# A hybrid decoder step: convolution output and sample unit moved into the chain over token tiles

## The chip, the cores and the metric

The kernel runs on one core of a Trainium2 chip. The metric is the device time of one execution in microseconds (us); of several runs the median counts. The engines are named as in the profile: PE is TensorE (matmuls; PEld its weight loads), DVE is VectorE, ACT is ScalarE, POOL is GpSimd, SP is SyncE, which here only issues DMAs.

## The reference

One inference step through two layers, for a prompt of 1024 tokens and for 8 sample sequences of 8 tokens that come with their own states. Everything is in float32; the model width is 1024.

```python
# layer 0
proj = x @ w_in                                   # 1024 -> 2816
u = value * sigmoid(gate)                         # half A: 512 channels
a = silu(layer_norm(causal_conv_31_taps(u) + b))
# half B: 8 heads of 64; token shift, low-rank decay, gates
for t in tokens:                                  # state S: 64 x 64 for each head
    S = S * w_t + (S @ a_t) * b_t + v_t * k_t
    o_t = S @ r_t
b = (group_norm(o) + bonus) * g
mix = concat(a, b) @ w_out
# layer 1
mix = causal means over 2, 4, 8, 16 tokens, minus x, then @ pool_w
# after each of the two
x = layer_norm(ALPHA * x + mix)
x = layer_norm(ALPHA * x + (silu(x @ wg) * (x @ wu)) @ wd)   # 1024 -> 2816 -> 1024
```

The outputs are x for both kinds of tokens and the new states of convolution, token shift, matrix S and pooling.

## The kernel before

The 1088 tokens are nine tiles, 0 to 7 with 128 prompt tokens each and 8 with the 64 sample tokens. A product in float32 is made of three matmuls on high and low parts, each operand being split into the two (`split`; `mm`, L75, issues a matmul). All engines but one take their order from an automatic planner that goes by priority, which is program order unless `high_priority` shifts it; TensorE's order is the planner's too in phase 1 and in the first part of phase 2, and from `manual_schedule` in `phase2` on it is program order. PSUM has four tags, mm, o, ch and tp, of two buffers each.

*Phase 1* (`phase1`, L219 to L388) makes the projection in 22 output tiles. Its sequence is `ORDER` (L180). An entry c0 to c3 is a convolution tile of two projections, gate (evicted by ScalarE) and value (evicted by VectorE, L293), and then 31 taps over 1024 prompt tokens on VectorE (L305 to L312), issued at a low priority (`LATE`); the few sample taps are products on POOL (L320) with a reduction on VectorE. The result goes to DRAM (`accd`, L323). The entries 20 and 21 are the low-rank inputs, 16 to 19 are v, 12 to 15 k, and 8 to 11 r, for the head pairs p0 to p3. When k and r of a pair are there, `prep` makes that pair's operands in three blocks of tokens, and `invert(p)` (L643 to L666) inverts the triangular matrices of the pair, in 31 steps of two instructions each, a product into `xt` and a sum into `X`. Its tiles have one buffer, so the four pairs are inverted one after another, p0 and p3 on POOL, p1 and p2 on VectorE (`PINV`). The result goes to DRAM.

*Phase 2* (`phase2`, L934 to L1027) turns this into the mixed output. The convolution's share is `convs`, eleven slots: slot x transposes tile x of `accd` and normalises it (`conv_a`, names `cl`, `cz`), makes the output product of tile x-2 with the upper half of `w_out` (`wout` with `wA`, names `wo`, `ahl`, `y`), and transposes back with the activation (`conv_b`, names `clt`, `yh`). The first eight slots are emitted ahead of the chain, under the planner's order for TensorE; three follow in units 0 to 2.

The chain goes over units 0 to 7, one for each prompt tile. `load_unit` brings a unit's operands from DRAM; `unit_pe` makes its transposes and merges the inverted blocks (the first is `pT`, L749); `chain` makes the dependent steps, two chunks of 64 tokens each, and between them calls `fill`, which takes further work for TensorE from the queue `fq`: the next unit's `unit_pe`, convolution slots, the step `gn` of the unit before (`gn_out`: group norm on VectorE, then gate), and tails. `tail(i)` is the output product of tile i with the lower half of `w_out` (`wB`, from the gated result `bt`) and the layer norm (`normalize`). `xt(i)` transposes a finished tile for the FFN. Units 3 to 7 take tails 0 to 5 and the `xt` of tiles 0 to 4. The sample's matrices are inverted by `invert(None)`, emitted after unit 0; `chain_sample` (four functions, s0 to s3, for each pair) begins in unit 7 and stands mostly behind it, together with tails 6, 7 and 8. `wB` is loaded after unit 2 with its split on POOL (L91). The nine `y` tiles stay in SBUF, and `xt` of tiles 7 and 8 is done beside the first FFN products.

After it come the FFN of layer 0, the pooling layer and its FFN, which are matmuls from weights that are streamed in.

Of the kernel before, what the change touches and what calls it, by code (L numbers as in the profile page):

```python
# [17 lines left out]
D = 1024  # L18
# [43 lines left out]
class Prog:  # L62
# [77 lines left out]
    def xt(self, l, i, y, pool, tag):  # L140
# [38 lines left out]
    CONV0 = 8  # L179
    ORDER = ("c0", "c1", 20, 21, 16, 12, 8, "c2", 17, 13, 9, "c3", 18, 14, 10, 19, 15, 11)  # L180
# [4 lines left out]
    CAUTO = 8  # L185
# [7 lines left out]
    def consts(self, es, e1):  # L193
        tc, nc, I = self.tc, self.nc, self.I
        pool = lambda name, bufs=1, **kw: es.enter_context(tc.tile_pool(name=name, bufs=bufs, **kw))
        self.pp = pool("psum", 2, space=PSUM)
# [8 lines left out]
        self.c1d = [[self.dr.tile([128, TH], F32, name=f"c1d{l}_{x}") for x in range(NF)] for l in range(2)]  # L205
        self.hd = [[self.dr.tile([128, TOK], F32, name=f"hd{l}_{f}") for f in range(NF)] for l in range(2)]
# [12 lines left out]
    def phase1(self):  # L219
# [13 lines left out]
        pool = lambda name, bufs=1, **kw: es.enter_context(tc.tile_pool(name=name, bufs=bufs, side="right", **kw))  # L233
# [38 lines left out]
        def conv_tile(ct):  # L272
# [33 lines left out]
            with tc.high_priority(offset=-self.LATE):  # L306
# [16 lines left out]
                nc.scalar.dma_start(out=self.accd[ct], in_=acc)  # L323
# [67 lines left out]
    def conv_a(self, i):  # L391
# [44 lines left out]
    def wout(self, i, get, w, alpha, after=None):  # L436
# [26 lines left out]
    def convs(self, wA):  # L463

        slots = []
        for x in range(11):
            out = []
            if x < 9:
                out += self.conv_a(x)
            if x >= 2:  # L470
                out += self.wout(x - 2, lambda j=x - 2: self.chl.pop(j), wA, ALPHA)
            if x < 9:
                out += self.conv_b(x)
            slots.append(out)
        return slots

# [191 lines left out]
    def load_unit(self, i):  # L668

        nc, up = self.nc, self.up  # L670
        u = type("Unit", (), {})()
        u.i, u.samp, u.nm = i, i == 8, f"t{i}"
# [7 lines left out]
        u.TT = up.tile([128, G, 64], F32, tag="TT", name=f"TT_{nm}")  # L680
# [8 lines left out]
        u.A21 = up.tile([128, G, 32], F32, tag="A21", name=f"A21_{nm}")  # L689
        u.ATm = [up.tile([128, G, 128], F32, tag=f"ATm{hd}", name=f"ATm{hd}_{nm}") for hd in range(2)]  # L690
# [49 lines left out]
    def merge(self, u):  # L740
# [5 lines left out]
        def one():  # L746
# [3 lines left out]
            t.T11 = up.tile([128, G, 32], F32, tag="T11", name=f"T11_{nm}", bufs=1)  # L750
# [92 lines left out]
    def gn_out(self, u, src, bts):  # L843
# [19 lines left out]
        def step():  # L863
# [12 lines left out]
            bts[u.i] = bt  # L876
        return step

    def chain_sample(self, u):
# [7 lines left out]
        S0, rS, w, pc = {}, {}, {}, {}  # L887
# [14 lines left out]
        def s1(p):  # L902
            pc[p] = self.psum("ch", f"spc{p}")
            for hd in range(2):
                self.mm(pc[p][H[hd], 0:64], ATm[hd][:, p, 0:64], SUV[:, 0, 0, hd, p])
            w[p] = self.wp_.tile([128, 4, 64], F32, tag="w", name=f"sw{p}")
            self.copy_act(w[p][:, 0], pc[p][:, 0:64])

        def s2(p):
            for hd in range(2):  # L910
                self.mm(pc[p][H[hd], 64:128], TTt[H[hd], p, :], w[p][H[hd], 0])
            self.copy_act(SUV[H[0], 0, 1, 0, p], pc[p][H[0], 64:128])
            nc.vector.tensor_copy(out=SUV[H[1], 0, 1, 1, p], in_=pc[p][H[1], 64:128])

        def s3(p):
            po = self.psum("o", f"spo{p}")
# [14 lines left out]

        return s0, s1, s2, s3, [Osb[:, hd].rearrange("p c v -> p (c v)") for hd in range(2)]

    def phase2(self):  # L934
        tc, nc, I, O = self.tc, self.nc, self.I, self.O
        es = ExitStack()
        pool = lambda name, bufs=1, **kw: es.enter_context(tc.tile_pool(name=name, bufs=bufs, side="right", **kw))
# [3 lines left out]
        self.tpool = pool("tmp2", 5)  # L941
# [22 lines left out]
        def xt(i):  # L964
            return self.xt(0, i, self.y[i], self.tpool, "t")

        self.fq, self.cz, self.chl = deque(), {}, {}
        bts, wB, gn = {}, [], {}
        wA = [self.load_w(I["w_out"][k], f"woA{k}", nc.vector) for k in range(4)]
        us = {0: self.load_unit(0), 1: self.load_unit(1)}  # L970
        slots = self.convs(wA)
        first = slots[:self.CONV0]
# [580 lines left out]
```

## Time and profile before

| | |
|---|---|
| Median of 3 runs | 2350.27 us (2343.52 to 2356.04) |
| Profiled execution | 2353.67 us, span 2351.9 us, mean granted clock 0.958 |
| PE busy | 2191.6 us, 93% of the span |
| PEld busy | 1971.6 us, 84% |
| DVE busy | 1558.9 us, 66% |
| ACT busy | 910.3 us, 39% |
| POOL busy | 449.3 us, 19% |
| DMA | 352.83 MB, mean 150 GB/s |

The span is the time from the first to the last instruction of the profiled execution; the busy times are sums over it. A busy share is an average over stages that have different limits, so it says little about a change in one stage. For that the stretch has to be cut out: busy time and granted clock in windows, and the order of the instructions of one engine with what ended each wait.

### The profile page before, as it was taken

How to read it: one execution, taken by the hardware profiler on the slowest of the kernel's cores; microseconds unless marked ns; L12 is line 12 of the kernel's file. 1: busy time of each engine (PE TensorE's matmuls, PEld its weight loads, DVE VectorE, ACT ScalarE, POOL GpSimd, SP SyncE). 2: the span in 40 equal slices, each digit the busy share in tenths (PEclk: the TensorE clock that was granted, in tenths of full speed). 3: DMA queues.
4: the chain of work that ended last, by engine and by line, in shares of the span. 5: the costliest groups of instructions: out<-in, count | busy, mean ns of one | idle time of the engine just before them, and what ended most of it. 6: DMA issues, size and time to landing. Idle time of an engine off the chain costs nothing.

```text
span 2351.9 us, 39322 instructions
## 1 busy us (share of the span) xinstructions
PE 2191.6 (93%) x15026; PEld 1971.6 (84%) x15026; DVE 1558.9 (66%) x2859; ACT 910.3 (39%) x2041; POOL 449.3 (19%) x551
## 2 busy tenths in 40 slices
PE   8898898869896899999999999989999999999998
PEld 7887787657664799999997787879999999977886
DVE  6987698734457535777767657455477777667565
ACT  3243244445642543333333434343443333334332
POOL 3588866563111000000000101000000000000010
PEclk9999899679998999999999999999999999999999
DMA  5132326745532654333348555444463333376662
GB/s 169 48 116 75 108 86 193 230 124 152 158 95 98 228 193 148 113 119 120 120 128 268 186 163 185 141 157 159 159 222 120 120 120 120 121 241 188 218 199 92
DMA packets 234362, 352.83 MB, mean 150 GB/s; under 512 B 73461, under 2 KB 151597, under 8 KB 234164
## 3 DMA queue, kind: packets, MB, share of 16 engines
q1 hardware_dynamic: 187294, 284.01, 39.1%
q10 hardware_dynamic: 46878, 66.30, 8.0%
q8 instruction: 118, 1.93, 0.3%
q14 instruction: 72, 0.59, 0.1%
HBM read 261.72 MB, written 88.74 MB: 149 GB/s over the span
## 4 chain that ended last, share of the span: by engine, by line
PE 60%; DVE 4%; DMA 4%; issue 2%; ACT 1%; SPq 0%; POOL 0%; ACTq 0%; POOLq 0%; DVEq 0%
PE dn L75 17%; DMA yr<-yd 1%; PE wo L75 1%; PE pp L75 1%; PE pl L75 1%; DMA b<-lnv 1%; PE pa_1u L75 1%; DVE op_d L96 1%; PE pa_10u L75 1%; PE pa_4g L75 1%; PE pa_2g L75 1%; PE pa_5g L75 1%; PE pa_3u L75 1%; PE pa_2u L75 1%; PE pa_3g L75 1%
## 5 line engine op out<-in xcount | busy, mean ns | idle before, releaser
L75 PE MATMUL dn<-op_d,h 128*128 128x512 f32 (+1 forms) x2288 | 544.7, 395 | 16.7 <-ACT op_d L72 6.6
L75 PEld LDWEIGHTS dn<-op_d,h 128*128 128x128 f32 (+1 forms) x2288 | 422.1, 187 | 117.9 <-DVE op_d L96 8.4
L75 PE MATMUL in<-xh,hl_in 128*128 128x384 f32 (+1 forms) x1056 | 282.5, 348 | 15.8 <-ACT xh L72 7.5
L104 POOL TENSOR_TENSOR rstd_f<-rs_f,mhalf 128x1 f32<-128x1 f32 (+1 forms) x18 | 36.3, 2017 | 1328.2 <-DVE rs_f L103 762.4
L96 DVE TENSOR_TENSOR op_d<-raw_d,op_d 128x512 fp32r<-128x512 f32 x264 | 179.2, 685 | 161.5 <-ACT op_d L72 161.0
L72 ACT ACTIVATE op_d<-raw_d 128x512 fp32r<-128x512 f32 x264 | 163.4, 625 | 292.4 <-PE dn L75 262.2
L75 PEld LDWEIGHTS in<-xh,hl_in 128*128 128x128 f32 x1056 | 199.0, 200 | 28.4 <-ACT xm L345 8.0
L312 DVE SCALAR_TENSOR_TENSOR acc<-u,hv,acc 128x1024 f32<-128x1024 f32 x120 | 193.2, 1619 | 0.8
L75 PE MATMUL in<-xl,hl_in 128*128 128x384 f32 (+1 forms) x528 | 182.7, 346 | 2.2 <-DVE xl L96 2.2
L75 PEld LDWEIGHTS in<-xl,hl_in 128*128 128x128 f32 x528 | 105.7, 200 | 5.4 <-DVE xl L96 2.9
L96 DVE TENSOR_TENSOR h<-hr,h 128x384 fp32r<-128x384 f32 (+2 forms) x176 | 72.8, 433 | 15.4 <-ACT h L72 15.4
L72 ACT ACTIVATE h<-hr 128x384 fp32r<-128x384 f32 (+2 forms) x176 | 69.2, 416 | 17.1 <-DMA hr<-hd 12.5
L156 ACT ACTIVATE xo<-xt,vec 128x128 f32<-128x128 f32 (+1 forms) x144 | 53.0, 452 | 44.1 <-PE xt L154 43.1
L75 PE MATMUL wo<-hl_woB,bhl 128*128 128x512 f32 (+1 forms) x216 | 65.0, 445 | 5.0 <-ACT bhl L72 4.9
L104 POOL TENSOR_TENSOR rstd_m<-rs_m,mhalf 128x1 f32<-128x1 f32 (+1 forms) x18 | 11.3, 629 | 271.2 <-DVE rs_m L103 264.7
L91 POOL TENSOR_TENSOR hl_in<-raw_in,hl_in 128x1024 fp32r<-128x1024 f32 x21 | 58.5, 2785 | 15.7 <-ACT hl_in L72 15.7
L75 PE MATMUL wo<-hl_woA,ahl 128*128 128x512 f32 (+1 forms) x216 | 57.6, 418 | 0.8 <-DVE y L456 0.4
L75 PEld LDWEIGHTS wo<-hl_woB,bhl 128*128 128x128 f32 (+1 forms) x216 | 41.2, 202 | 18.5 <-ACT bhl L72 6.0
L75 PEld LDWEIGHTS wo<-hl_woA,ahl 128*128 128x128 f32 (+1 forms) x216 | 40.6, 194 | 11.1 <-DVE y L456 0.7
L72 ACT ACTIVATE rw<-in 128x384 f32<-128x384 f32 (+2 forms) x56 | 22.0, 394 | 46.1 <-PE in L75 30.9
L75 PE MATMUL pl<-hl_pw,phl 128*128 128x256 f32 (+1 forms) x216 | 33.4, 286 | 3.3 <-DVE phl L96 2.8
L320 POOL TENSOR_TENSOR prod<-u,hv 128x496 f32<-128x496 f32 x16 | 30.6, 1915 | 29.9 <-DVE u L293 16.3
(1040 smaller groups left out, 4769.8 us busy)
## 6 DMA issues: line engine op xcount, KB each, us to landing
raw_d<-ffn_down SPq DMA_DIRECT2D x132, 512.0 KB, 3.8
hd<-sg ACTq DMA_DIRECT2D x88, 272.0 KB, 4.1
hr<-hd SPq DMA_DIRECT2D x88, 192.0 KB, 3.7
raw_in<-w_in SPq DMA_DIRECT2D x22, 512.0 KB, 4.3
xl<-xtd SPq DMA_DIRECT2D x16, 544.0 KB, 4.6
ATm_t<-atd SPq DMA_DIRECT2D x16, 512.0 KB, 5.3
yr<-yd SPq DMA_DIRECT2D x16, 512.0 KB, 5.7
xtd<-xo ACTq DMA_DIRECT2D x28, 256.0 KB, 3.7
```

The source lines that it names most:

```text
L72: self.nc.scalar.activation(out=out, in_=in_, func=AF.Copy)
L75: self.nc.tensor.matmul(out, lhsT, rhs, start=start, stop=stop, **kw)
L91: (eng or nc.gpsimd).tensor_tensor(out=hl[:, 1, :], in0=raw, in1=hl[:, 0, :].bitcast(F32), op=ALU.subtract)
L96: (eng or self.nc.vector).tensor_tensor(out=out_lo, in0=src, in1=out_hi.bitcast(F32), op=ALU.subtract)
L104: nc.gpsimd.tensor_tensor(out=out, in0=t[:P, :n], in1=self.mhalf[:P, :n], op=ALU.pow)
L156: nc.scalar.activation(out=xo[:, k, :n], in_=ps[:, k * 128:k * 128 + n], func=AF.Identity, scale=self.v("lng", 16 * l + 4 * q + k), bias=s ...
L312: nc.vector.scalar_tensor_tensor(out=out, in0=src, scalar=cw(j), in1=out, op0=ALU.mult, op1=ALU.add)
L320: nc.gpsimd.tensor_tensor(out=prod, in0=win, in1=taps, op=ALU.mult)
```

## The change

- `ORDER` puts c1 behind the tiles of p0 and c3 last. The store of `accd` is issued from SP instead of ACT.
- No slot of `convs` is emitted ahead of the chain. `SLOTS` puts two slots into unit 1 and three into each of units 2, 3 and 4; `manual_schedule` begins before the first unit, and `invert(None)` stands first.
- `y` has four buffers in place of nine tiles: after the convolution's share a tile is stored to DRAM (`store_y`) and read back before its tail (`load_y`); the gated `bt` goes the same way.
- The sample unit has its own buffers and is loaded in unit 0. Its transposes, s0, and s1 to s3 stand in units 4, 5 and 6, with s1 and s2 joined over the four pairs; its group norm is made in unit 7.
- `TAILS` and `XTS` place tail 0 in unit 5, tails 1 and 2 in unit 6, 3 and 4 in unit 7; behind the chain follow `gn[7]` and the tails 5, 8, 6, 7 with the `xt` of the other tiles between. `xt` of tile 8 is no longer beside the FFN.
- `wB` is loaded before unit 5, its split on VectorE. Some pools get `reuse_waits="tile"`, and `tmp2` has six buffers for five.

The diff, cut to its core:

```diff
-    ORDER = ("c0", "c1", 20, 21, 16, 12, 8, "c2", 17, 13, 9, "c3", 18, 14, 10, 19, 15, 11)
+    ORDER = ("c0", 20, 21, 16, 12, 8, "c1", 17, 13, 9, "c2", 18, 14, 10, 19, 15, 11, "c3")
...
-                nc.scalar.dma_start(out=self.accd[ct], in_=acc)
+                nc.sync.dma_start(out=self.accd[ct], in_=acc)
...
-                out += self.wout(x - 2, lambda j=x - 2: self.chl.pop(j), wA, ALPHA)
+                out += self.wout(x - 2, lambda j=x - 2: self.chl.pop(j), wA, ALPHA, lambda j=x - 2: self.store_y(j))
...
+    def load_y(self, i):
+        n = TT_TILES[i][1]
+        self.y[i] = self.ypool.tile([128, D], F32, tag="y", name=f"yb{i}")
+        self.nc.sync.dma_start(out=self.y[i][:n], in_=self.yad[i][:n])
+        self.bt[i] = self.bp.tile([128, 4, n], F32, tag="bt", name=f"bl{i}")
+        self.nc.sync.dma_start(out=self.bt[i], in_=self.btd[i][:, :, :n])
...
-            bts[u.i] = bt
+            nc.sync.dma_start(out=self.btd[u.i][:, :, :n], in_=bt)
...
+        def s1():
+            x["pc"] = self.psum("tp", "spc")
+            for p in range(4):
+                for hd in range(2):
+                    self.mm(x["pc"][H[hd], p * 64:(p + 1) * 64], ATm[hd][:, p, 0:64], SUV[:, 0, 0, hd, p])
...
+        self.man.enter_context(tc.manual_schedule(engines={mybir.EngineType.PE}))
+        self.invert(None, self.sp)
+        self.fq.extend(self.unit_pe(us[0]))
         self.fill(1e9)
+        for i in range(8):
+            if 1 <= i < 7:
+                us[i + 1] = self.load_unit(i + 1)
+            if i == 0:
+                us[8] = self.load_unit(8, "s")
+                S0, S12, S3, out = self.chain_sample(us[8])
+            if i == 5:
+                wB.extend(self.load_w(I["w_out"][4 + k], f"woB{k}", nc.vector) for k in range(4))
+            for j in self.TAILS[i]:
+                self.load_y(j)
+            work = [x for j in self.SLOTS[i] for x in slots[j]]
+            work += [x for j in self.TAILS[i] for x in tail(j)]
+            work = work[:2] + [x for j in self.XTS[i] for x in xt(j)] + work[2:]
+            if 4 <= i < 7:
+                work = mix(work, [self.unit_pe(us[8]), S0, S12 + S3][i - 4])
+            if i == 7:
+                gn8 = self.gn_out(us[8], out)
+                work = [(1.4, gn8)] + work
+            work = work[:self.GNAT] + [(1.4, lambda i=i: gn[i - 1]())] * (i > 0) + work[self.GNAT:]
+            if i < 7:
+                work = mix(work, self.unit_pe(us[i + 1]))
+            self.fq.extend(work)
+            self.chain(us[i], us[i + 1] if i < 7 else None, lambda po, i=i: gn.update({i: self.gn_out(us[i], po)}))
+        self.fill(2.5)
+        self.fq.append((1.4, lambda: gn[7]()))
+        last = None
+        for j in (5, 8, 6, 7):
+            self.load_y(j)
+            t = tail(j)
+            self.fq.extend(t[:2] + (xt(last) if last else xt(3) + xt(4)) + t[2:])
             self.fill(1e9)
+            last = j
...
+    SLOTS = ((), (0, 1), (2, 3, 4), (5, 6, 7), (8, 9, 10), (), (), ())
+    TAILS = ((), (), (), (), (), (0,), (1, 2), (3, 4))
+    XTS = ((), (), (), (), (), (), (0,), (1, 2))
...
-                for i in (7, 8):
-                    self.side.extend(f for _, f in self.xt(0, i, self.y[i], self.rawp, "rw"))
+                self.side.extend(f for _, f in self.xt(0, 7, self.rawp, "rw"))
```

## Rows read from the trace of the kernel before

**Rows 1.** Windows: window, length; busy PE, PEld, DVE, ACT, POOL; clock, DMA, GB/s.

```profile
401.10:504.50 103.40, 72.81 (x308) 57.14 (x307) 68.56 (x154) 44.32 (x110) 71.24 (x147) 0.74 0.73 216
504.50:512.70 8.20, 6.16 (x81) 4.86 (x81) 0.00 (x0) 6.07 (x15) 6.29 (x24) 0.50 0.24 53
512.70:529.50 16.80, 15.74 (x210) 12.44 (x209) 5.23 (x12) 10.62 (x29) 2.50 (x5) 0.89 0.36 95
529.50:552.50 23.00, 22.73 (x276) 17.73 (x276) 10.25 (x38) 11.29 (x30) 4.70 (x6) 0.78 0.43 119
552.50:572.90 20.40, 19.05 (x277) 13.92 (x277) 10.56 (x38) 14.28 (x31) 12.23 (x10) 1.00 0.72 200
572.90:598.70 25.80, 25.22 (x300) 19.17 (x300) 13.13 (x43) 11.23 (x29) 8.59 (x10) 1.00 0.45 132
598.70:626.30 27.60, 23.18 (x296) 17.86 (x294) 12.40 (x42) 16.41 (x43) 5.13 (x7) 0.94 0.59 161
626.30:652.40 26.10, 21.75 (x287) 16.68 (x286) 12.94 (x43) 13.54 (x35) 5.13 (x7) 0.95 0.52 144
...
677.50:697.50 20.00, 18.08 (x231) 14.02 (x230) 11.71 (x41) 11.14 (x31) 3.38 (x4) 1.00 0.41 100
697.50:758.20 60.70, 48.83 (x276) 28.67 (x272) 43.88 (x119) 15.07 (x46) 9.47 (x9) 0.86 0.21 72
```

**Rows 2.** Timeline, POOL: start, length, instruction, [idle before]; last inversion's first, last.

```profile
462.60 0.24 POOL L662 TENSOR_TENSOR xt<-X,At 128x31 f32<-128x31 f32 x1 [3.27 <-DMA X<-xinitP]
...
496.86 0.24 POOL L664 TENSOR_TENSOR X<-X,xt 128x16 f32<-128x16 f32 x1
```

**Rows 3.** Timeline, PE: the chain's first transposes.

```profile
504.53 1.09 PE L749 MATMUL pT_t<-ident,TT_t 128*128 128x128 f32 x4 [9.95 <-POOL xt_None L662]
```

**Rows 4.** Timeline, DVE: the last value evictions of c0 and of c1.

```profile
35.93 0.55 DVE L293 SCALAR_TENSOR_TENSOR u<-u,in 128x256 f32<-128x256 f32 x2 [3.03 <-PE in L75]
...
64.54 0.55 DVE L293 SCALAR_TENSOR_TENSOR u<-u,in 128x256 f32<-128x256 f32 x2
```

**Rows 5.** Timeline, POOL: one product of `prep`, in p0 and in p3.

```profile
131.69 1.89 POOL L558 TENSOR_TENSOR AR_p0b<-xm,Wp_p0b 128x384 f32<-128x384 f32 x1 [0.55 <-DVE xm L346]
...
395.12 0.92 POOL L558 TENSOR_TENSOR AR_p3b<-xm,Wp_p3b 128x384 f32<-128x384 f32 x1 [1.38 <-DVE xm L346]
```

**Rows 6.** Groups by form, 60 to 500 us: count | busy us, mean ns | idle before.

```profile
L312 DVE SCALAR_TENSOR_TENSOR acc<-u,hv,acc 128x1024 f32<-128x1024 f32 x110 | 174.0, 1592 | 0.6
...
L91 DVE TENSOR_TENSOR hl_woA<-raw_woA,hl_woA 128x1024 fp32r<-128x1024 f32 x4 | 5.7, 1415 | 0.0
```

**Rows 7.** Timeline, POOL: inversion steps of p0 (first two rows) and of p3.

```profile
199.56 1.34 POOL L662 TENSOR_TENSOR xt<-X,At 128x56 f32<-128x56 f32 x1
...
221.19 0.41 POOL L664 TENSOR_TENSOR X<-X,xt 128x126 f32<-128x126 f32 x1
...
466.69 0.32 POOL L662 TENSOR_TENSOR xt<-X,At 128x78 f32<-128x78 f32 x1
...
467.49 0.36 POOL L662 TENSOR_TENSOR xt<-X,At 128x100 f32<-128x100 f32 x1
```

**Rows 8.** Groups, PE, 406 to 497 us.

```profile
L75 PE MATMUL wo<-hl_woA,ahl 128*128 128x512 f32 x144 | 36.2, 410 | 0.8 <-DVE y L456 0.4 <-DVE ATm_p3b L612 0.4
...
L425 PE MATMUL clt<-ident,cz 128*128 128x128 f32 x32 | 6.8, 351 | 5.1 <-DVE cz L410 5.1
L402 PE MATMUL cl<-ident,ac 128*128 128x128 f32 x32 | 6.4, 334 | 4.2 <-DMA ac<-accd 4.2
```

**Rows 9.** Groups by form, 690 to 740 us: the sample's products and reductions.

```profile
L898 DVE TENSOR_REDUCE rS<-sm 128x64 f32<-128x512 f32 x8 | 7.9, 1010 | 0.1
...
L896 DVE TENSOR_TENSOR sm<-sar,c_smask 128x512 f32<-128x512 f32 x8 | 5.2, 678 | 0.0
```

**Rows 10.** Timeline, DVE: group norm of unit 7.

```profile
707.19 1.13 DVE L852 BATCH_NORM_STATS2 gst_t<-po_t 128x6 f32<-128x64 f32 x8
...
710.84 2.10 DVE L860 TENSOR_SCALAR on_t<-po_t,gmv_t,grs_t 128x64 f32<-128x64 f32 x8 [1.51 <-POOL grs_t L104]
```

More of the change, by code (lines that the diff above doesn't have):

```diff
@@ L205, in consts @@
         self.c1d = [[self.dr.tile([128, TH], F32, name=f"c1d{l}_{x}") for x in range(NF)] for l in range(2)]
+        self.yad = [self.dr.tile([128, D], F32, name=f"yad{i}") for i in range(9)]
+        self.btd = [self.dr.tile([128, 4, 128], F32, name=f"btd{i}") for i in range(9)]
         self.hd = [[self.dr.tile([128, TOK], F32, name=f"hd{l}_{f}") for f in range(NF)] for l in range(2)]
@@ L688, in load_unit @@
             nc.sync.dma_start(out=u.TT[r0:r0 + 32, :, b * 32:b * 32 + 32], in_=src)
-        u.A21 = up.tile([128, G, 32], F32, tag="A21", name=f"A21_{nm}")
-        u.ATm = [up.tile([128, G, 128], F32, tag=f"ATm{hd}", name=f"ATm{hd}_{nm}") for hd in range(2)]
+        u.A21 = up.tile([128, G, 32], F32, tag="A21" + tag, **kw, name=f"A21_{nm}")
+        u.ATm = [up.tile([128, G, 128], F32, tag=f"ATm{hd}" + tag, **kw, name=f"ATm{hd}_{nm}") for hd in range(2)]
         for hd in range(2):
@@ L900, in s0, with s2 @@
                 self.copy_act(SUV[H[hd], 0, 0, hd, p], rs[0:64, :])
[L902 to L913, printed above, removed]
+        def s1():
[3 more added lines that the diff above has]
+                    self.mm(x["pc"][H[hd], p * 64:(p + 1) * 64], ATm[hd][:, p, 0:64], SUV[:, 0, 0, hd, p])
+            x["w"] = self.wp_.tile([128, 4, 64], F32, tag="w", name="sw")
+            self.copy_act(x["w"].rearrange("p a b -> p (a b)"), x["pc"][:, 0:256])
+        def s2():
+            pc = x["pc"]
+            for p in range(4):
+                for hd in range(2):
+                    self.mm(pc[H[hd], 256 + p * 64:256 + (p + 1) * 64], TTt[H[hd], p, :], x["w"][H[hd], p])
+            self.copy_act(SUV[H[0], 0, 1, 0].rearrange("p a b -> p (a b)"), pc[H[0], 256:512])
+            nc.vector.tensor_copy(out=SUV[H[1], 0, 1, 1].rearrange("p a b -> p (a b)"), in_=pc[H[1], 256:512])
         def s3(p):
-            po = self.psum("o", f"spo{p}")
+            po = self.psum("tp", f"spo{p}")
             for hd in range(2):
@@ L964, in xt @@
         def xt(i):
-            return self.xt(0, i, self.y[i], self.tpool, "t")
-        self.fq, self.cz, self.chl = deque(), {}, {}
-        bts, wB, gn = {}, [], {}
+            return self.xt(0, i, self.tpool, "t")
+        self.fq, self.cz, self.chl, self.bt = deque(), {}, {}, {}
+        wB, gn = [], {}
+        us = {0: self.load_unit(0), 1: self.load_unit(1)}
         wA = [self.load_w(I["w_out"][k], f"woA{k}", nc.vector) for k in range(4)]
-        us = {0: self.load_unit(0), 1: self.load_unit(1)}
         slots = self.convs(wA)
-        first = slots[:self.CONV0]
-        rest = [[x for j in js for x in slots[j]] for js in np.array_split(np.arange(self.CONV0, 11), 3)]
         def mix(a, b):
@@ L1369, in build @@
             self.phase1()
-            ypool = ey.enter_context(tc.tile_pool(name="y", bufs=1, side="right"))
-            self.y = [ypool.tile([128, D], F32, name=f"y{i}") for i in range(9)]
-            self.wring.append(ew.enter_context(tc.tile_pool(name="wring2", bufs=2, side="right")))
+            self.ypool = self.pool(ey, "y", 4, side="right")
+            self.y = {}
+            self.wring.append(self.pool(ew, "wring2", 2, side="right"))
             self.phase2()
@@ L1426, in finish @@
                                 steps += self.pool_tile(i) + late
[L1427 removed]
+                                late = [f for _, f in self.xt(1, i, self.xop, "t")]
                             steps += [lambda: None] * 3 + late
```

99 lines of the change are left out of this document (31 added, 68 removed).

## The prediction

> **What bounds the kernel now.** I read the busy time by stage first, then the planner's order inside the stretch that the change touches, engine by engine, and last what each wait there ended on. From the second half on, TensorE works with hardly a gap and nothing is edited there; so the change is decided before 758 us. The windows [rows 1] cut that part. In the first, 401.1 to 504.5 us, the projections are done, the chain has not begun, and TensorE is busy 72.81 of 103.4 us at a granted clock of 0.74: a hole, held open by the last triangular inversion and filled with eight convolution slots. The windows that follow are the chain, the first unit's transposes and then unit by unit (unit 6, like unit 5, is left out): TensorE busy 19 of 20 us in unit 2, 25.2 of 25.8 in unit 3, and from there on at clock 0.94 or more. The reader is to see that the chain is close to TensorE's own pace, and the hole is not. The last window, 60.7 us, holds the sample unit and three tails: TensorE 48.83 at clock 0.86, VectorE 43.88. I leave that as the second place where time is lost.
>
> What ends the hole is a queue of inversions: `invert` has one buffer per tile, so heads p0 to p3 follow one another. The last one runs on POOL from 462.60 to 497.10 [rows 2], its result goes through DRAM, and the first transposes of the chain start at 504.53 [rows 3]. I call that moment T0; from T0 to the end of the last tail (758.2) are 253.7 us.
>
> **The change, part by part.** The sum is made against the profiled execution: 2353.67 us, of which the span is 2351.9; it lies 3.4 above the median of three runs, 2350.27, and what the sum gives is added to that median.
>
> *Order of the projections: T0 moves forward.* The convolution tile c1 no longer stands ahead of p0's group, and each group after it keeps its neighbours. The value evictions of c0 end at 36.5, those of c1 at 65.1 [rows 4]: 28.6 us, all of which the queue of inversions gains. Beside that, c1's 31 taps no longer run while p0 is prepared. POOL's 128x384 product took 1.89 us then, and 0.92 without taps [rows 5]; two of p0's three blocks have seven such steps each on their path, 14 x 0.97 = 13.6. I take 10, bounds 0 (VectorE still has c0's taps) and 20 (the evictions also wait less).
>
> Against it stands what is late next. c3's taps now come last, beside the last inversion, which in the kernel before had no taps beside it. Shifted by 38.6, that inversion starts at 424. Tile 11 is projected by 401.1 - 38.6 = 362.5, c3 takes 28.6 more, so taps start at 391; 31 of 1.59 us [rows 6] are 49. VectorE's 68.56 us in the hole [rows 1] are by an estimate half convolution, half p2's inversion and p3's preparation; of that second half some 15 fall after 391. So the taps last until about 455. So 31 us of the inversion lie under taps. A pair of its instructions there costs 2.1 us: from 199.56 to 221.60 p0's inversion made eight, with 5.1 us of other POOL work between [rows 7]. Without taps a pair is 0.80 (466.69 to 467.49, its two rows plus the step to the next) [rows 7], and over the whole last inversion 1.11 (34.5/31, the sample's own inversion interleaved in its second half) [rows 2]. 31/2.1 = 15 pairs at 1.0 more: +15. Bounds: 0 (taps done in time) and +31 (all 31 pairs). Moving the sample's inversion ahead can interleave it with more pairs; the six small convolution roots leave POOL there; I let the two cancel, bounds -3 and +10.
>
> T0 moves by 28.6 + 10 - 15 = 23.6, to 481. Ends: 28.6 + 0 - 31 - 10 = -12 (later) and 28.6 + 20 + 3 = 52.
>
> *The convolution moves from the hole into the chain.* What had filled the hole is 144 output matmuls in 36.2 us, six tiles' worth of 6.0, and eight pairs of transposes in 13.2, or 1.65 a slot [rows 8]. Nothing takes their place but c3's projections, which are over by 391; from there to 481 TensorE has only p3's preparation. Now the chain, window by window, from [rows 1]. The window of 20.4 less one output part is a unit's base, 14.4. The two tails of the next window agree: 14.4 + 12.0 = 26.4 against 25.8. One pair of `xt` steps costs (27.6 - 14.4 - 6.0)/2 = 3.6. Then:
> - unit 0's own transposes: 8.2, as before.
> - unit 0: only unit 1's transposes fill it, 16.8 - 6.0, so 11.
> - unit 1: 23.0 - 6.0 + 2 x 1.65 = 20.
> - units 2 and 3, three slots each: 14.4 + 18.0 + 5.0 = 37.4, twice (before 20.4 and 25.8).
> - unit 4: 14.4 + 18.0 + 1.65 + half of a unit's transposes at full clock (8.2 x 0.50 / 2 = 2) = 36.
> - unit 5: one tail and the sample's first step. VectorE: 10.6 of a unit's own, eight mask products and reductions of 1.69 [rows 9] = 13.5, the tail's rest 3 by an estimate; and the four weight splits, which leave POOL for VectorE, 5.7 [rows 6]: 32.8 against 23 on TensorE. Some of it can start in unit 4: 30.
> - unit 6: two tails, one `xt`, the sample's rest (16 matmuls of 512 columns at 0.25 and 48 small ones, an estimate 7): 14.4 + 12.0 + 3.6 + 7 = 37.
> - unit 7: 14.4 - 4.1 + 1.5 + 12.0 + 7.2 = 31.
> - after it: unit 7's outputs and gates about 6; TensorE's order is written out, so it waits for `gn[7]`, whose statistics begin at 707.19 and end at 712.94 [rows 10], 5.8; four tails 24; five `xt` with nothing but tails beside them, half of 3.6 each, 9: 44.8.
>
> The sum is 292.8, 39.1 more than 253.7. The gain in it is the last stretch, 60.7 to 44.8, and the sample's work no longer standing alone. The ends: 278, if units 2 to 4 run at the base's pace with nothing for the transposes' evictions, unit 5 takes TensorE's 23 and the wait for `gn[7]` is covered; 305, if each of units 2 to 7 stalls by 2 more, since `cl`, `clt`, `xt` and the unit's own transposes share two PSUM buffers.
>
> At unit 5 a rule bears on this. The Trainium skill, "Perfetto Trace Analysis", section Optimization Strategy, says that a kernel whose regimes have different most-contended engines can gain from interleaving them; VectorE's sample beside TensorE's chain is such a pair. By it unit 5 would be 23 and the sum of the parts 7 less. The sum keeps 30, since in [rows 1] units with `xt` steps cost 3.6 for each of them with no engine full.
>
> *Traffic.* Nine `y` and nine `bt` tiles go to DRAM and back, 36 more DMAs on SP; the store of `accd` moves there from ACT. The DMA share in the chain is 0.36 to 0.72 [rows 1], and a tail's reload is issued a unit ahead. Cost 0; without that cover one late reload stops TensorE for some 5 us (the page's landing times, 3.6 to 5.7). `xt(8)` leaves the first FFN products: -1.
>
> *Sum:* -23.6 + 39.1 - 1 = +14.5: 2350.27 + 14.5 = 2365.
>
> **Rivals.**
> 1. *Faster: the inversion runs free of the taps.* Place: POOL between p2's and p3's results. For it: p2's inversion may end earlier without convolution slots on VectorE, and the planner puts taps last. Against: taps last is where they meet the last inversion. T0 moves by 48.6, the chain takes 278 (+24.5): 2350.3 - 48.6 + 24.5 - 1 = 2325. At a chain of 293 it decides from the point where the first transposes start before 455: 504.5 - (39.1 - 1 + 11.8) = 454.6.
> 2. *Even: the exchange comes out.* The taps end before the inversion begins, T0 moves by 38.6, the chain is as forecast: 2350.3 - 38.6 + 39.1 - 1 = 2350. For it: 28.6 is sure, and so is that clock 0.74 in the hole left something to win.
> 3. *Slower still: the hole only moves.* All 31 pairs meet a tap: T0 moves by 28.6 - 31 = -2: 2350.3 + 2 + 39.1 - 1 = 2390. By the Trainium skill, "GPSIMD Engine Reference", section Specifications, GpSimd shares its SBUF interfaces with VectorE and contends with instructions of two SBUF inputs; the taps are such, and so are the inversion pairs on VectorE. Against it: 49 us of taps that begin 33 us before the inversion cannot cover all of it unless they slow down too.
> 4. *The change does not do what it says:* c3 last in program order need not be last on TensorE, whose order in that phase is the planner's. If its matmuls fill earlier gaps, the taps come earlier, which is rival 2.
>
> **How the numbers follow.** Forecast 0.40, with its own range 2357 to 2376; rival 3, 0.14; rivals 2 and 4, 0.22; rival 1, 0.24. What a measurement of this kernel can tell from no change is about 0.5%, 11.8 us: slower starts at 2362. Three quarters of the forecast lie above it. Slower 0.31 + 0.14 = 0.45, same 0.09 + 0.22 = 0.31, faster 0.24. The range runs from just above rival 1 (2328) to just above rival 3 (2394).
>
> **What would show it.** T0: the first `pT` transposes at 481, with clock under 0.7 on TensorE from about 391. POOL's inversion pairs of p3 at over 2 us while `acc` taps run, at under 1.2 after. Units 2 to 4 at 36 to 38 us, unit 5 bound by VectorE, 44 to 46 from the end of unit 7 to the last output matmul. The prediction is wrong if T0 comes before 455, or if T0 to the last tail takes under 275.

## The result, and the profile after

The changed kernel takes 2441.32 us (median of 4 runs, 2432.84 to 2449.05) against 2353.15 for the kernel before (4 runs): a ratio of 1.0383, 95% interval 1.0356 to 1.0411, 88 us slower. The profiled execution is the fastest of its four, 2432.84 us with a span of 2431.0, so its windows are somewhat shorter than those of a median run.

The windows answer to [rows 1], with the same columns: c3's projections, the hole, unit 0's transposes, units 0 to 7, and what stands behind the chain.

```profile
407.00:432.60 25.60, 25.60 (x144) 25.40 (x144) 3.61 (x10) 3.67 (x9) 9.74 (x26) 0.93 0.58 169
432.60:485.70 53.10, 0.06 (x1) 0.00 (x0) 41.25 (x37) 0.88 (x3) 44.89 (x47) 0.52 0.53 143
485.70:493.90 8.20, 6.16 (x82) 4.86 (x82) 0.00 (x0) 6.08 (x15) 0.00 (x0) 0.50 0.24 53
493.90:512.40 18.50, 12.52 (x178) 10.09 (x177) 7.07 (x10) 11.66 (x27) 1.74 (x3) 0.59 0.49 138
512.40:552.40 40.00, 23.86 (x270) 19.41 (x270) 14.76 (x46) 16.22 (x41) 26.03 (x72) 0.56 0.56 165
552.40:596.80 44.40, 38.12 (x350) 28.99 (x349) 20.15 (x57) 18.36 (x47) 6.77 (x10) 0.88 0.52 153
596.80:641.40 44.60, 38.21 (x351) 29.04 (x350) 20.86 (x57) 20.56 (x54) 6.22 (x9) 0.89 0.48 144
641.40:686.00 44.60, 37.21 (x377) 26.47 (x376) 20.99 (x52) 24.58 (x61) 6.17 (x7) 0.92 0.54 171
686.00:716.40 30.40, 26.29 (x295) 16.61 (x294) 22.44 (x55) 12.82 (x34) 8.76 (x10) 1.00 0.46 132
716.40:757.50 41.10, 36.74 (x385) 25.31 (x386) 28.30 (x84) 15.97 (x41) 5.20 (x7) 0.96 0.42 135
757.50:793.80 36.30, 28.31 (x244) 21.69 (x241) 16.76 (x61) 11.29 (x32) 5.55 (x6) 0.86 0.36 108
793.80:843.30 49.50, 38.56 (x213) 27.01 (x212) 21.04 (x59) 17.07 (x47) 3.80 (x5) 0.90 0.43 131
```

T0 is 485.8, 18.7 earlier. From there to the last tail are 357.5 us, in place of 253.7: +103.8. What follows is 6.0 shorter. Together -18.7 + 103.8 - 6.0 = 79.1, the difference of the two spans.

The hole is still there, with no TensorE work in it. POOL's timeline (it answers to [rows 2] and [rows 7]) and VectorE's say why it lasts:

```profile
421.22 0.24 POOL L676 TENSOR_TENSOR xt<-X,At 128x31 f32<-128x31 f32 x1 [13.97 <-DMA X<-xinitP]
...
467.07 1.23 POOL L678 TENSOR_TENSOR X<-X,xt 128x70 f32<-128x70 f32 x1
468.37 1.20 POOL L676 TENSOR_TENSOR xt<-X,At 128x56 f32<-128x56 f32 x1
469.65 1.26 POOL L678 TENSOR_TENSOR X<-X,xt 128x56 f32<-128x56 f32 x1
...
477.52 1.26 POOL L678 TENSOR_TENSOR X<-X,xt 128x16 f32<-128x16 f32 x1
```

```profile
452.20 27.80 DVE L314 SCALAR_TENSOR_TENSOR acc<-u,hv,acc 128x1024 f32<-128x1024 f32 x21
500.91 0.43 DVE L839 COPY SUV_t<-pc_t 64x256 f32<-64x256 f32 x1 [20.91 <-ACT SUV_t L72]
501.37 2.60 DVE L314 SCALAR_TENSOR_TENSOR acc<-u,hv,acc 128x1024 f32<-128x1024 f32 x2
```

p3's inversion takes 57.6 us, 34.5 before. It runs at its old pace until c3's taps begin at 434. Beside the 21 taps of the row above, 1.32 us each, every instruction of it takes 1.20 to 1.27, whatever its size; from 434 to 452 some meet a tap, and four products of c3's sample taps stand between them on POOL. And VectorE's queue holds a chain step in front of the last two taps: c3's result is complete at 504, not 483.

In unit 1 TensorE's written order puts the transposes `clt` of a normalised convolution tile `cz` ahead of the next chain step, and they wait:

```profile
523.00 1.12 PE L75 MATMUL ps_t<-SUV_t,BKT_t 128*64 128x64 f32 x16
534.38 1.09 PE L428 MATMUL clt<-ident,cz 128*128 128x128 f32 x4 [10.25 <-DVE cz L413]
```

```profile
529.49 0.28 POOL L676 TENSOR_TENSOR xt_None<-X_None,At_s 64x60 f32<-64x60 f32 x1
529.74 1.63 POOL L104 TENSOR_TENSOR grs_t<-rs_gt,mhalf 128x8 f32<-128x8 f32 x1
531.34 0.55 POOL L104 TENSOR_TENSOR crs<-rs_c,mhalf 128x1 f32<-128x1 f32 x1
```

`cz` needs `crs`, the reciprocal root of its norm. The input of `crs` is there at 525.2, but POOL makes it at 531.3, behind the first 23 of the 62 steps of the sample's inversion, which ran from 520.9 to 549, and behind `grs_t`, the same root for the group norm.

Unit 3 shows what a wait costs besides its length:

```profile
604.87 1.67 PE L75 MATMUL wo<-hl_woA,ahl 128*128 128x512 f32 x6
609.79 1.90 PE L881 MATMUL pgn_t<-ident,on_t 128*128 128x128 f32 x4 [3.26 <-DVE on_t L875]
611.49 1.92 PE L75 MATMUL pg_t<-sdg,c_g 128*128 128x128 f32 x8
613.05 4.16 PE L75 MATMUL wo<-hl_woA,ahl 128*128 128x512 f32 x12
...
776.65 0.60 PE L881 MATMUL pgn_t<-ident,on_t 128*128 128x128 f32 x4
777.09 1.06 PE L75 MATMUL pg_t<-sdg,c_g 128*128 128x128 f32 x8
```

Here TensorE waits for `on_t`, the chain's output after the group norm on VectorE. After 3.26 us idle the next two groups take 1.90 and 1.92 us, at a granted clock of 0.50 (609.8 to 613.0); the same two in unit 7, with no wait, take 0.60 and 1.06, at 1.00. The twelve products behind them take 4.16, against 2 x 1.67 for the last row ahead of the wait.

### The profile page after: what moved, and what is told of

Read it like the earlier page. It is cut to its first block, busy times and chain, and to the rows that moved or that the text cites. A ratio compares the mean times of both kernels' runs of the same rounds, so it can differ in the third digit from the quotient of the medians.

```text
span 2431.0 us, 39370 instructions
## 1 busy us (share of the span) xinstructions
PE 2204.2 (91%) x15026; PEld 1977.5 (81%) x15026; DVE 1558.8 (64%) x2860; ACT 911.4 (37%) x2035; POOL 434.1 (18%) x547
## 4 chain that ended last, share of the span: by engine, by line
PE 67%; DVE 12%; POOL 6%; DMA 6%; issue 4%; ACT 3%; SPq 1%; POOLq 0%; ACTq 0%; DVEq 0%
PE dn L75 17%; PE wo L75 3%; DVE acc L314 3%; PE in L75 3%; POOL X L678 2%; POOL xt L676 2%; PE pp L75 1%; PE pl L75 1%; DVE xt L676 1%; DVE X L678 1%; PE po_t L75 1%; DMA xl<-xtd 1%; DMA yr<-yd 1%; PE pc_t L75 1%; PE xt L155 1%
## 5 line engine op out<-in xcount | busy, mean ns | idle before, releaser
L104 POOL TENSOR_TENSOR rstd_f<-rs_f,mhalf 128x1 f32<-128x1 f32 (+1 forms) x18 | 34.5, 1918 | 1324.6 <-DVE rs_f L103 760.8
L314 DVE SCALAR_TENSOR_TENSOR acc<-u,hv,acc 128x1024 f32<-128x1024 f32 x120 | 185.9, 1550 | 1.9
L96 DVE TENSOR_TENSOR h<-hr,h 128x384 fp32r<-128x384 f32 (+2 forms) x176 | 72.7, 432 | 14.1 <-ACT h L72 14.1
L157 ACT ACTIVATE xo<-xt,vec 128x128 f32<-128x128 f32 (+1 forms) x144 | 52.4, 465 | 53.6 <-PE xt L155 52.8
L75 PE MATMUL wo<-hl_woA,ahl 128*128 128x512 f32 (+1 forms) x216 | 62.9, 435 | 0.3 <-DVE ya L459 0.2
L764 PE MATMUL pT_t<-ident,TT_t 128*128 128x128 f32 x34 | 7.4, 353 | 58.3 <-DMA TT_t<-dxp 53.1
L676 POOL TENSOR_TENSOR xt<-X,At 128x126 f32<-128x126 f32 (+22 forms) x62 | 43.0, 693 | 18.4 <-DMA X<-xinitP 14.0
```

What stands on the lines that cost most here:

```text
L75: self.nc.tensor.matmul(out, lhsT, rhs, start=start, stop=stop, **kw)
L96: (eng or self.nc.vector).tensor_tensor(out=out_lo, in0=src, in1=out_hi.bitcast(F32), op=ALU.subtract)
L104: nc.gpsimd.tensor_tensor(out=out, in0=t[:P, :n], in1=self.mhalf[:P, :n], op=ALU.pow)
L157: nc.scalar.activation(out=xo[:, k, :n], in_=ps[:, k * 128:k * 128 + n], func=AF.Identity, scale=self.v("lng", 16 * l + 4 * q + k), bias=s ...
L314: nc.vector.scalar_tensor_tensor(out=out, in0=src, scalar=cw(j), in1=out, op0=ALU.mult, op1=ALU.add)
L676: eng.tensor_tensor(out=xs, in0=X[:P, :m, s:s + 1].to_broadcast([P, m, w]), in1=At[:P, s:s + 1, s + 1:].to_broadcast([P, m, w]), op=ALU.mult)
```

## The experiments

All ratios are against the kernel before, whose median was 2353.2 to 2353.6 in these sessions.

**e1_warm**, work in the hole:

```diff
+        keep = self.psum("mm", "keep")
+        for _ in range(50):
+            self.mm(keep, self.ident, self.sdg[:, 0:512])
         self.fq.extend(self.unit_pe(us[0]))
```

> The changed kernel with 50 extra float32 products of 128x512 on TensorE between c3's projections and the first pT (they read sdg and the identity, their result is read by nobody). Theory 'clock': the hole of 53 us without TensorE work (432.6 to 485.7, clock 0.52) is why units 0 and 1 run at 0.59 and 0.56; with work there they start near full clock, their 36 us of busy time shrink by about 15, and the time falls from 2441 to about 2426. Theory 'waits': units 0 and 1 are held by results of VectorE, ScalarE and POOL that TensorE's written order waits for; the clock rises, the two units stay within 4 us of 58.5, and the time stays within 6 us of 2441.

2426.03 us, ratio 1.0309 [1.0276, 1.0341]. The time is the one that "clock" gave, but by luck, since units 0 and 1 don't show it: the hole ran at 0.94, and unit 0 at 0.50 all the same. The run is no clean refutation, since the products ended 10.8 us before T0 (53.6 - 42.86) and TensorE idled until then.

```profile
425.30:478.90 53.60, 42.86 (x100) 18.63 (x99) 43.30 (x39) 0.88 (x3) 45.41 (x47) 0.94 0.53 142
478.90:487.00 8.10, 6.12 (x80) 4.86 (x80) 0.00 (x0) 6.36 (x15) 0.00 (x0) 0.50 0.46 135
487.00:507.10 20.10, 14.05 (x178) 10.91 (x177) 5.74 (x9) 12.44 (x30) 4.78 (x16) 0.50 0.85 261
```

From T0 to the last tail it took 362.8 us, no less than without the extra products. What moved was T0, to 478.9, and the sample's inversion, to 501 to 529; unit 1 took 33.6 us, not 40. The 7 us at T0 arose in phase 1, ahead of the extra products: p1's inversion began at 262.5, and at 269.7 in the changed kernel. Why this median is 15 us lower stays open; the two profiled runs differ by 3.

**e2_order**, the old `ORDER` alone:

```diff
-    ORDER = ("c0", 20, 21, 16, 12, 8, "c1", 17, 13, 9, "c2", 18, 14, 10, 19, 15, 11, "c3")
+    ORDER = ("c0", "c1", 20, 21, 16, 12, 8, "c2", 17, 13, 9, "c3", 18, 14, 10, 19, 15, 11)
```

> The changed kernel with the old ORDER (c1 second, c3 before p2's tiles), everything else of the change kept. My theory: the new order moved the first pT forward by 19 us (504.5 to 485.8) but took away the free VectorE of the last inversion; with the old order the inversion of p3 has no taps beside it (34 us, not 57), and begins some 35 us later: first pT at 490 to 500, time 2441 + 5 to 15 = 2446 to 2456. Rival: c3 last costs more than it brings, since its last two taps, the weight split for the convolution's output and the first convolution slots wait for it: time under 2430.

2443.04 us, 1.0395 [1.0366, 1.0423]: level with the changed kernel, a little under my 2446. T0 is 500.0, and from there to the last tail it is 353.0 us, against 357.5 in the changed kernel's fastest run and 365.2 in e4 below, which does the same work. So the order brings 14 us at T0, and the chain gives back 4.5 to 12 of them in these traces; the medians are level. T0 lies between 478.9 and 487.3 in the six traces with the new order, and at 497.4 (e10) and 500.0 in the two with the old one and no slot ahead of the chain.

**e3_ahead**, eight slots ahead of the chain again:

```diff
+        for x in slots[:8]:
+            self.fq.extend(x)
+        self.fill(1e9)
         self.man.enter_context(tc.manual_schedule(engines={mybir.EngineType.PE}))
...
+    SLOTS = ((8,), (9,), (10,), (), (), (), (), ())
+    TAILS = ((), (), (), (0, 1), (2,), (3,), (4,), (5,))
```

> The changed kernel with the old ORDER, eight convolution slots emitted ahead of the chain again, slots 8 to 10 in units 0 to 2, and tails and xt placed in the units as before; what stays of the change is the sample unit in units 4 to 6, y and bt through DRAM, wB's split on VectorE, and tails 8, 6, 7 at the end. Theory 'slots': the loss of 88 us is the convolution slots inside the chain; here it is gone, 2340 to 2360. Rival 'sample and traffic': the sample's work inside the chain or the y traffic costs a good part; 2380 or more.

2364.02 us, 1.0045 [1.0027, 1.0064]: 4 above the range of "slots" and far from that of its rival. Against e2 it is 79 us less, of a loss of 88. With the slots the tails go forward too, and `wB` is loaded in unit 3, not 5. One window each from T0 to the last tail, of the kernel before, of this one, and of e2 with the slots in the chain:

```profile
504.50:758.20 253.70, 222.73 (x2502) 162.51 (x2502) 131.75 (x409) 123.17 (x321) 62.36 (x88) 0.90 0.42 119
```

```profile
504.30:772.30 268.00, 231.78 (x2510) 168.33 (x2510) 136.74 (x411) 123.68 (x321) 51.94 (x76) 0.87 0.50 147
```

```profile
500.00:853.00 353.00, 291.34 (x2718) 213.12 (x2718) 166.63 (x470) 151.78 (x393) 57.10 (x90) 0.84 0.43 130
```

Eight slots add 85.0 us to the chain, 59.6 of them TensorE's busy time (7.4 a slot) and 25.4 idle time. With them ahead of the chain T0 is 504.3, and 500.0 without.

**e4_inv_late**, the sample's inversion emitted in unit 3:

```diff
-        self.invert(None, self.sp)
...
-            if i == 0:
+            if i == 3:
+                self.invert(None, self.sp)
                 us[8] = self.load_unit(8, "s")
```

> The changed kernel with the sample's inversion, its load and chain_sample emitted in unit 3 and not ahead of the chain. In the changed kernel POOL makes the sample's inversion from 521 to 549, inside unit 1, and the two rsqrt of unit 1 (for cz and the group norm) stand in its queue behind part of it; TensorE waits 10.25 us for cz there. Theory 'POOL queue': unit 1 shrinks from 40 to about 27 and the time to about 2428. Rival: the wait moves with the inversion into unit 3 or is replaced by the next late result; within 5 us of 2441.

2442.91 us, 1.0373 [1.034, 1.0406]. Inconclusive: POOL's order is the planner's, and the inversion still ran in unit 1, from 525 to 554, when its input buffer had come free behind the last split of `wA` at 522. The only evidence for the queue on POOL is that e1 and e2, where it ran earlier, have unit 1 at 33.6, this kernel at 37.6 and the changed one at 40: 4 to 6 us. The wait for `cz` is 4.8 and 4.0 there, and 9.0 and 10.3 here and in the changed kernel.

**e5_gn_late**, group-norm steps later in the written order (`GNAT` is the place of the step in a unit's list of further work):

```diff
-    GNAT = 3
+    GNAT = 8
...
-                work = [(1.4, gn8)] + work
+                work = work[:5] + [(1.4, gn8)] + work[5:]
...
-        self.fq.append((1.4, lambda: gn[7]()))
+            ... xt(3) + xt(4) + [(1.4, lambda: gn[7]())] ...
```

> The changed kernel with the group-norm steps later in TensorE's written order: GNAT 8 for 3, the sample's (gn8) five steps into unit 7, gn[7] behind half of tail 5. The steps wait for on_t of VectorE, 15.7 us in seven waits, and once more 5.6 us (pg). Theory 'waits in the written order': these 21 us go, little comes in their place, 2441 - 15 to 21 = 2420 to 2426. Rival: the chain has little spare work, so that the wait moves to the next late result (cz, crs, PSUM buffers); 2435 to 2445.

2425.65 us, 1.0306 [1.0279, 1.0333]: 16 us, as the waits gave. But not where I thought: units 2 to 4 only fell to 43.7, 43.6 and 42.3; in unit 3 a wait of 2.7 for `cz` took the place of the 3.3. From unit 7's start to the last tail it is 73.3 us against 86.

**e6_fill**, extra products inside units 0 and 1:

```diff
+            if i < 2:
+                def extra():
+                    ps = self.psum("mm", f"ex{self.uid()}")
+                    for _ in range(2):
+                        self.mm(ps, self.ident, self.sdg[:, 0:512])
+                work = mix(work, [(1.3, extra)] * 6) if work else [(1.3, extra)] * 6
```

> The changed kernel with 24 extra float32 products of 128x512 on TensorE (results read by nobody), two at a time among the filler work of units 0 and 1. The first run with extra products showed that a busy hole does not keep the clock up in units 0 and 1 (0.50 and 0.60 all the same), so theory 'own work': the clock is low there because these units hold only small products and waits. Then the extra 20 us of work (0.86 each at full clock, by the 50 that took 42.9 us) lift the clock to 0.8 or more in unit 1, and the time rises by less than half of them: under 2451. Rival 'it only adds': units 0 and 1 grow by 20 to 35, time 2460 or more.

2442.24 us, 1.0369 [1.0346, 1.0392]: 24 more products cost nothing, as "own work" had it. Units 0 and 1:

```profile
494.90:514.60 19.70, 19.65 (x201) 10.98 (x200) 8.32 (x10) 10.51 (x24) 2.85 (x3) 0.94 0.34 102
514.60:557.80 43.20, 29.76 (x295) 19.13 (x294) 15.63 (x47) 17.90 (x45) 25.41 (x72) 0.80 0.58 176
```

Unit 0 is 19.7 long with TensorE full and 18.5 with it a third idle, unit 1 43.2 for 40: the extra products went into waits, and the length of these units was not the sum of TensorE's work. Unit 0 can't be shorter than the chain's dependent steps. In the changed kernel its second chunk, with nothing between the steps, takes 7.5 us (504.86 to 512.39); by an estimate from this two chunks take 15 at the clock there.

**e7_order_b**, in the kernel before, c1 behind p0's tiles, c2 behind p1's, c3 behind p2's:

```diff
-    ORDER = ("c0", "c1", 20, 21, 16, 12, 8, "c2", 17, 13, 9, "c3", 18, 14, 10, 19, 15, 11)
+    ORDER = ("c0", 20, 21, 16, 12, 8, "c1", 17, 13, 9, "c2", 18, 14, 10, "c3", 19, 15, 11)
```

> The kernel before with one part of the new order alone: c1 behind p0's tiles, c2 behind p1's, c3 behind p2's (not last). My theory: the inversions all start up to 28 us earlier, c3's taps end before the last inversion, and the eight slots still fit into the hole: first pT at 480 to 490, time 2353 - 15 to 25 = 2328 to 2338. Rival: the eight slots wait for c3's taps and TensorE's written order begins behind them, so the hole ends with the slots: first pT about 505 or later, time 2350 to 2365.

2390.49 us, 1.0163 [1.0129, 1.0198]: wrong, and past the rival too. p0's inversion began 38 us earlier (157, not 195), but p2's ended no earlier (453; 454 before): it took 86 us for 51, with c3's taps between its steps on VectorE until 433. Then p3's, which began at 462.6 in the kernel before [rows 2], began at 492.7. Its start values `X` are loaded from DRAM, and SP issues that load 29 us later than in the kernel before, behind loads for the sample (`S`). Here, and then before:

```profile
484.79 2.54 SPq L891 DMA_DIRECT2D S<-state_wkv  x4
487.37 0.43 SPq L657 DMA_DIRECT2D X<-xinitP  x1
```

```profile
458.08 0.36 SPq L657 DMA_DIRECT2D X<-xinitP  x1
```

On POOL:

```profile
482.70 0.54 POOL L104 TENSOR_TENSOR crs<-rs_c,mhalf 128x1 f32<-128x1 f32 x1 [20.60 <-DVE rs_c L103]
...
492.67 0.23 POOL L662 TENSOR_TENSOR xt<-X,At 128x31 f32<-128x31 f32 x1
```

From the issue of the load to the first step are 5.3 us, and 4.5 before, where POOL stood idle until `X` came. So SP's queue explains the 30 us. POOL had the slots' `crs` ahead of the step as well, but when it stood idle for them, the load of `X` had not been issued. T0 was 539.

**e8_wb**, e3 with `wB` loaded behind unit 2, split on POOL:

```diff
-            if i == 3:
-                wB.extend(self.load_w(I["w_out"][4 + k], f"woB{k}", nc.vector) for k in range(4))
+            if i == 2:
+                wB.extend(self.load_w(I["w_out"][4 + k], f"woB{k}") for k in range(4))
```

> The kernel with eight slots ahead again (2364 us), and wB loaded behind unit 2 with its split on POOL as in the kernel before. There TensorE waited 8.7 us in unit 3 in front of an output product. Theory: that wait was for the split of wB, queued in VectorE; it goes, 2353 to 2357. Rival: it was for a y tile that comes back from DRAM; 2361 to 2367.

2367.22 us, 1.006 [1.0044, 1.0076]: no change. I had put the wait into the wrong place: in e3 it ends at 495.6, in the last slot ahead of the chain, and here it is still there (9.5 us, until 498.3). It is for `ya`, one of the `y` tiles.

**e9_sample_end**, e3 with the sample behind the chain:

```diff
-            if 4 <= i < 7:
-                work = mix(work, [self.unit_pe(us[8]), S0, S12 + S3][i - 4])
...
+        t = tail(6)
+        self.fq.extend(S0[2:] + t[:1] + S12[:1] + t[1:2] + S12[1:] + t[2:3] + S3[:2] + t[3:] + [(1.4, lambda: gn[7]())] + S3[2:])
```

> The kernel with eight slots ahead (2364 us), and the sample unit placed behind the chain as in the kernel before; what is left of the change is y and bt through DRAM, wB's place, and the extra buffers. It tells what of the remaining 11 us is the sample's move. Theory 'the sample inside the chain costs what it cost alone, and the queue around it': 2353 to 2358, so the traffic is worth 5 or less. Rival 'traffic': 2362 to 2370, the sample's move is worth nothing.

2378.18 us, 1.0092 [1.0058, 1.0127]: above both ranges, and by the medians 14 above e3, though the two intervals just overlap. T0 is 512.1, and from there to the last tail it is 278.1 us, 10.1 more than in e3. In it TensorE waits twice for a reload of `bt` that nothing covers any more (6.6 and 7.5 us, for its split `bhl`). Waits from 455 to 830 us, with total, count and longest:

```profile
PE wo L75 <- ACT bhl L72: 14.1, 2, 7.5
PE wo L75 <- DVE ya L459: 10.4, 2, 9.9
```

The wait of 9.9 us for `ya`, in the last slot ahead of the chain, is no part of the difference: e3 has 8.75 there, with T0 at 504.3. T0 comes later here mostly because phase 1, the same code, was later. p1's inversion began so in e3 and in e9:

```profile
304.73 1.94 DVE L676 TENSOR_TENSOR xt<-X,At 128x31 f32<-128x31 f32 x1
```

```profile
310.69 1.95 DVE L676 TENSOR_TENSOR xt<-X,At 128x31 f32<-128x31 f32 x1
```

p3's ended 7.0 us later. What makes phase 1 differ, and what the four `y` buffers do to the wait for `ya`, was not tried.

**e10_early**, old `ORDER`, late group norm, slots from unit 0 on:

```diff
+    SLOTS = ((0, 1, 2), (3, 4, 5), (6, 7), (8, 9), (10,), (), (), ())
+    TAILS = ((), (), (), (), (0,), (1,), (2,), (3, 4))
```

> The changed kernel with the old ORDER (2443 us), the later group norm (worth 16 us), and the slots spread from unit 0 on: 3, 3, 2, 2, 1, tails 0, 1, 2 in units 4 to 6, 3 and 4 in unit 7. Units 0 and 1 took 20 us of extra products for nothing, so theory 'units 0 and 1 have free TensorE time': 2443 - 16 - 20 = about 2407, clock of units 0 and 1 above 0.8. Rival: the slots only lengthen units 0 and 1 by what they save later; 2425 or more.

2408.64 us, 1.0232 [1.0205, 1.026]: the time is as expected, the clock of unit 0 is not (0.67, where I had 0.8 or more; unit 1 has 0.85). Units 0 and 1 grew to 29.0 and 45.4 us, with six slots in them for two. Units 0 and 3, and T0 to last tail:

```profile
505.50:534.50 29.00, 22.05 (x227) 17.20 (x226) 11.76 (x24) 16.18 (x42) 4.08 (x8) 0.67 0.36 96
...
611.60:638.30 26.70, 25.46 (x310) 19.73 (x309) 13.36 (x44) 15.85 (x44) 5.60 (x7) 1.00 0.63 196
```

```profile
497.40:811.90 314.50, 271.81 (x2718) 199.62 (x2718) 167.50 (x470) 151.35 (x393) 56.85 (x89) 0.90 0.48 146
```

The same 2718 matmuls as in e2 take 19.5 us less busy time and 19 less idle time. Against e3, the eight slots cost 46.5 us here, 40.0 of them busy time.

**e11_p3_dve**, p3's inversion on VectorE (`PINV = (0, None)`).

> The changed kernel with p3's inversion on VectorE in place of POOL. On POOL it took 57.6 us, of 34.6 in the kernel before, with pairs of 2.6 us beside taps and 0.9 without. Theory: on VectorE it stands ahead of the taps and takes about 25 to 40, first pT at 455 to 470; but c3's taps end as much later, and unit 1 waits for them: time 2441 - 0 to 10. Rival: T0's gain goes through whole, 2420 or less.

2436.84 us, 1.0343 [1.0311, 1.0375]. The time is in the range, T0 is not: 485.8, as in the changed kernel. On VectorE the planner alternates inversion steps with taps, and the inversion runs from 419.7 to 477.6, 58 us again:

```profile
446.46 1.27 DVE L314 SCALAR_TENSOR_TENSOR acc<-u,hv,acc 128x1024 f32<-128x1024 f32 x1
447.66 0.27 DVE L678 TENSOR_TENSOR X<-X,xt 128x120 f32<-128x120 f32 x1
447.85 1.27 DVE L314 SCALAR_TENSOR_TENSOR acc<-u,hv,acc 128x1024 f32<-128x1024 f32 x1
```

**e12_ahead_gn**, e8 with the group-norm edit of e5.

> The kernel with eight slots ahead and wB as before (2367 us), with the group-norm steps later as in the run that won 16 us. Its waits for on_t are 8.5 and 5.7 us. Theory: most of these 14 us go: 2350 to 2356, level with the kernel before. Rival: these units are full of TensorE work and a wait that goes is replaced; 2361 to 2368.

2373.51 us, 1.0071 [1.0047, 1.0095]: above both ranges, no gain. From T0 to the last tail it is 269.5, as in e3 (268.0). T0 is 512.7, and 506.1 in e8; 4.5 us of that difference lie in phase 1, where the last inversion ended at 500.9, and at 496.4 in e8.

No version beat the kernel before.

## Why the prediction was wrong

*T0* was nearly right: 485.8 for 481. The queue of inversions gained what was forecast: p0's began 38.2 us earlier, for 28.6 + 10. The last one began at 421.2 (forecast 424) and took 57.6 us for 49.5. c3's projections came from 407 to 432.6, not by 391, so the inversion lay beside taps from 434 to its end, not for its first 31 us. The reason for the early start was incomplete, though: in e7 p0's inversion began as early, and p2's ended no earlier, with c3's taps beside it; in the changed kernel it ended at 408.4. e2 prices the whole order: 14 us at T0, nothing in the time.

*The chain* is the step that failed: 292.8 forecast, 357.5 measured. Its terms: unit 0 18.5 for 11, unit 1 40 for 20, units 2 to 4 44.4, 44.6, 44.6 for 37.4, 37.4 and 36, unit 5 30.4 for 30, unit 6 41.1 for 37, unit 7 36.3 for 31, the end 49.5 for 44.8. 50 of the 65 us lie in units 0 to 4. Of these 50, 42 are time in which TensorE stood idle, and 8 are busy time above the forecast.

The price of a slot in TensorE time was not the error: 7.4 us (e3 against e2), and 5.0 where the clock was higher (e3 against e10), for 7.65. The error was to treat a unit as a sum of TensorE times, with the waits of TensorE's written order at nothing. In units 0 and 1 I subtracted a slot's products from windows of [rows 1], in which TensorE was nearly full, and let the unit shrink by as much. What was left did not keep TensorE busy: 6.0 us of unit 0 and 16.1 of unit 1 were idle, 10.3 of these for `cz`, and the clock was 0.59 and 0.56. e6 shows that these two units could take 24 more products for 4.4 us more length. The forecast of 11 also lies below the estimate of 15 for unit 0's dependent steps; how short unit 1 can be was not measured. In units 2 to 4 I added three slots and no idle time. Their busy time came out near the forecast, 38.1, 38.2 and 37.2; on top came 6.3, 6.4 and 7.4 us idle, since results that TensorE's written order waits for (`on_t`, `crs`) come too late. In unit 3 of e10, with two slots and hardly a wait, the forecast's own terms, 14.4 + 2 x 6.0 + 1.65 (only one of these two slots has transposes) = 28, were met: 26.7. My upper end of 2 us a unit for such stalls was a third of what they are.

*The last stretch* was to gain 15.9 us and gained 11.2, and the sample's work was to cost 22.1 less in all (39.1 less eight slots of 7.65). e3 has the slots out of the chain, and there the rest of the change costs 14.3 from T0 to the last tail. How this divides between sample, traffic and tails stays open: e9 took the sample out of the chain and lost 14.1 us in waits for `bt`. I had priced a late reload at 5 us; the two in e9 took 6.6 and 7.5.

*The rule at unit 5* comes from "Perfetto Trace Analysis", section Optimization Strategy, of the Trainium skill: interleaving regimes with different busiest engines may improve a kernel. By it I had 23 there, and 30 in the sum; measured 30.4, with TensorE busy 26.3 and VectorE 22.4. The 30 was met by luck: it came from 32.8 us of VectorE work, and VectorE had 22.4 there (the four weight splits had been done in unit 4). Neither engine was full, so VectorE did not bound it.

*Rivals.* "The hole only moves" came nearest, at 2390, but in the number only: by it T0 moves by 2 us, and it moved by 18.7. No rival joined an emptied hole to a chain that cannot take its work at the hole's price. *The range* was short at the top by 47 us: its upper end, 305 for the chain, was made of stalls of one kind only. Two small slips bear on nothing: unit 6 of the kernel before ran at clock 0.92, not 0.94 or more, and 278 is 24.3 above 253.7, not 24.5.

## What to carry to other kernels

Work that fills a hole beside a serial bound costs little there (T0 504.3 with the eight slots, 500.0 without); moved into a chain that is near TensorE's pace it costs its full time, plus the waits of its own side steps (85 us). Before a unit is priced by subtraction, see whether TensorE's work sets its length: run it with extra work, and see whether it grows. An earlier start of one stage is worth only what the last stage of that queue gains, and a queue in which other entries stand ahead of that stage (SP's loads in e7) can hand all of it back. One profiled run of each kernel is little for a few microseconds: the same phase 1 began p1's inversion anywhere from 304.7 to 310.7 in six traces.

## What the hardware showed

- POOL's inversion steps took 0.23 to 0.47 us without taps (421 to 434, one of 1.34 apart) and 1.20 to 1.27 beside VectorE's taps of 1.32, one step for each tap. The Trainium skill, "SBUF — State Buffer", section "SBUF: two separate sides", says that a VectorE instruction with two SBUF inputs and a GpSimd instruction that reads SBUF share a port pair, which the first of them holds as an exclusive lock for its whole instruction. These rows agree: a tap has two such inputs.
- Work in the hole did not raise TensorE's granted clock in the unit behind it. In e1, after 42.9 us of products in the hole (clock 0.94) and 10.8 us idle, it was 0.50, the lower of its two levels, in unit 0's transposes and still in the 20.1 us of unit 0. In e6, with no work in the hole and the extra products inside unit 0, it was 0.94 there.
- A wait cost TensorE more than its length. In unit 3, behind 3.26 us idle, the clock was 0.50, and two groups took 3.82 us that took 1.66 in unit 7 without a wait.
